# Full-row second score product and token-ordered values in a hybrid attention layer

## The chip, the cores and the metric

The kernel runs on one core of a Trainium2 chip. The metric is the device time of one execution in microseconds (us). Inputs are float32; every large matrix product is carried out in a split form, in which a float32 operand is written as a high and a low part of the type float32r.

## The reference

One layer of a bidirectional encoder over 1024 tokens of width 1024. What matters here is the middle line, a mixture of dilated windows in three groups of eight heads (group 0: dilation 1, group 1: dilation 4, group 2: dilation 16).

```python
h = rmsnorm(x, attn_norm_g)
proj = h @ w_in                        # 1024 x 8096, split into the parts below
(c_q, c_kv, k_rope, z_mla, q_dil, k_dil, v_dil, z_dil, g_mla, g_dil) = jnp.split(proj, ...)
a_out = mla_attention(c_q, c_kv, k_rope, ...)            # 8 heads, dense
d_out = dilated_mixture(q_dil, k_dil, v_dil, positions)  # 3 x 8 heads of 64
merged = sigmoid(g_mla + b) * ((a_out * silu(z_mla)) @ w_o_mla) \
       + sigmoid(g_dil + b) * ((d_out * silu(z_dil)) @ w_o_dil)
return rmsnorm(x + merged @ w_out, final_norm_g)

# a dilated group: token t belongs to class t % dilation and sees, within its class,
# keys at most window / (2 dilation) = 64 places away
def to_sub(t):
    return t.reshape(B, L, dilation, H, D).transpose(0, 2, 3, 1, 4)
s = einsum('brhnqd,brhnkd->brhnqk', qb, kb) * D ** -0.5
p = exp(where(valid, s, NEG_INF) - max)                  # den = sum(p), o = p @ v / den
```

The three groups' outputs are then added with the weights of a softmax over their log-denominators.

## The kernel before

**Split products.** `split` makes the high part by a copy on ScalarE and the low part by a subtraction on VectorE or GpSimd. `mm3` (lines 67 to 71) adds three matmuls, high by high, low by high and high by low; wherever it is used, the profile has rows of L69, L70 and L71. Transposed normalised inputs stay in SBUF as `hT_h` and `hT_l`, 128 partitions x 8 chunks x 1024 tokens each. `dma` (line 65) issues every transfer from SyncE's queue, so all of them are rows of SP and L65, in one order.

**Order.** The program is written as functions, one after the other, and a scheduler with a timeline model places the instructions of each engine by the tiles that they read and write. Inside the attention the order is also written out: `feed` takes so many steps of a generator of other products, `fillers` (the z tiles, the gates and the branches' projections), and sets them behind the latest matmul of the attention (`self.anchor`). `FIRST_FEED` and `FEED` are the tables of these numbers.

**Stages, by the profiled execution.**
- 0 to 40 us: `latent_proj` loads the input and makes the latents; `token_factors` makes the norm's factor of each token, as a row in DRAM (`s_rs`) and back in columns (`rcol`, and by class of four `rcol4`).
- about 50 to 266 us: `dil_v`, the values of the dilated heads, for three groups of two "quads" of four heads each. A tile is 128 tokens by 256 columns: eight chunks of the contraction, three matmuls each, with the tokens as the weights of TensorE and the 256 columns of `wv` as the moving operand. In group 1 the 128 tokens of a tile are those of one class, every fourth column of `hT_h` and `hT_l`, so that the rows come out by class. ScalarE and VectorE scale the result into a tile `dv_st` (three buffers), and a store of 128 pieces of 2 KB takes it to DRAM (`s_dv`). Group 0 runs until about 112 us, group 1 until 218, group 2 until 266. Between them stand the steps of `latents`, the up-projections of the MLA branch, which go through two buffers in PSUM (`pl`) and two in SBUF (`mla_st`).
- 266 to 530 us: `dil_qk`, rotated queries and keys, stored in DRAM as `s_dq` and `s_dk`, with a high and a low part for groups 0 and 1.
- 532 to 876 us: `dil_attention`, in four pairs of heads; in each pair, two heads of group 0, two of group 1 (`dil_head`), and both heads of group 2 together (`dil_classes`), then `combine`. "Change of pair" below means the place where a pair's group 2 ends and the next pair's group 0 begins.
- 876 to 1250 us: the MLA attention, 1250 to 1397 us: the output projection.

**A head of group 0 or 1** loads three operands, each in two buffers: the queries `op_b` (two parts, high and low, of 64 rows x 1024 tokens), the keys `op_a` (the high part in rows 0 to 63, the low part in rows 64 to 127) and the values `op_c`. The high part of the queries is copied by ScalarE from rows 0 to 63 into rows 64 to 127 (line 628), so that one matmul over 128 rows (line 641) gives high queries times both parts of the keys. A second one (line 642) over 64 rows adds low queries times high keys. Both have 128 queries as weights and 256 keys as moving columns. There are 16 heads with 8 blocks of queries: 128 pairs of line 641 and line 642. `soft_block` then takes mask, maximum and exponential on VectorE (line 613) and ScalarE (line 614); line 649 transposes the result, and line 662 (group 0) or 670 (group 1) multiplies by the values.

Of the kernel before, what the change touches and what calls it, by code (L numbers as in the profile page):

```python
# [10 lines left out]
F32 = mybir.dt.float32  # L11
# [18 lines left out]
# steps of other products given between those of the attention  # L30
FIRST_FEED = 19
FEED = (1.9, 1.35, 1.2, 1.25, 2, 3, 1.1, 1.1)
# numbers of buffers
# [4 lines left out]
# column tiles of w_in that come out transposed  # L38
# [11 lines left out]
class Net:  # L50
# [22 lines left out]
    def split(self, raw, h, l, sub):  # L73
        """raw float32 -> h + l, both of float32r, exactly."""
        self.nc.scalar.copy(out=h, in_=raw)  # L75
        sub.tensor_tensor(out=l, in0=raw, in1=h.bitcast(F32), op=ALU.subtract)  # L76

# [10 lines left out]
    def proj_half(self, w, half, pool):  # L88
        """One column tile times 512 tokens: [128, 512] in PSUM."""
        return run_all(self.proj_steps(w, half, pool))  # L90

    def proj_steps(self, w, half, pool):
        """proj_half in steps of a chunk of the contraction."""
        ps = pool.tile([128, 512], F32, name="pj")
        t = slice(half * 512, half * 512 + 512)
        for kc in range(8):
            self.mm3(ps, w[0][:, kc], w[1][:, kc], self.hTh[:, kc, t], self.hTl[:, kc, t], kc == 0, kc == 7)
            if kc < 7:
                yield
        return ps  # L100

# [10 lines left out]
    def rsqrt(self, x, scale, pool, n):  # L112
        """(x * scale + EPS) ** -0.5 of [128, n], by Newton's method from the exponent's half."""
# [12 lines left out]
    def rsqrt_half(self, x, pool):  # L126
        """(2 x) ** -0.5 of [128, 1], with its sign turned: a step of Newton's method from the square root."""
        v = self.nc.vector
        y, u = (pool.tile([128, 1], F32, name=f"rs_{c}") for c in "yu")
        self.nc.scalar.activation(out=y, in_=x, func=AF.Sqrt, scale=2.0)  # L130
        v.reciprocal(out=y, in_=y)
        v.scalar_tensor_tensor(out=u, in0=y, scalar=x, in1=y, op0=ALU.mult, op1=ALU.mult)
        v.scalar_tensor_tensor(out=y, in0=u, scalar=-1.5, in1=y, op0=ALU.add, op1=ALU.mult)
        return y

    def load_x(self, half, kc, xp):
        """(x g)^T in two parts; the tokens' factors are applied to the products."""
# [8 lines left out]
    def latent_proj(self, lp, wl, xp, pj):  # L146
        """c_q, c_kv and the shared rotary key by token, before their factors, and the sums of squares."""
# [33 lines left out]
    def token_factors(self, xp, pp):  # L181
        """The input norm's factor of each token: in columns, by class of four, and on all partitions."""
# [15 lines left out]
        self.dma(self.rcol4, flat.rearrange("(k m r) -> m r k", k=2, r=4))  # L198

    def tables(self, tp):  # L200
        """cos and sin: rows p % 32 of the dilated heads' angles, rows p % 16 of MLA's."""
# [26 lines left out]
    def rope(self, pa, pb, cos, sin, tp):  # L228
        """Rotated halves of [128, 512] from two PSUM tiles."""
# [22 lines left out]
    def latents(self, up, lp, tp, pj):  # L252
        """The latents' norms and the up-projections, by 512 tokens."""
# [3 lines left out]
        for half in range(2):  # L257
            c512 = slice(half * 512, half * 512 + 512)
            # with the tokens' factors r: r * (r r mean + eps) ** -0.5
# [24 lines left out]
            # the shared rotary key: halves at rows 0..15 and 32..47  # L284
# [25 lines left out]
            # queries  # L310
# [6 lines left out]
            # keys  # L317
# [7 lines left out]
            # values  # L325
# [10 lines left out]
    def dil_v(self, g, quad, tp, pj):  # L336
        """Values of four dilated heads, by token (of groups 1 and 2, by class)."""
# [10 lines left out]
        for t in range(8):  # L348
            ps = pj.tile([128, 512], F32, name="pj")[:, :256]
            for kc in range(8):  # L350
                wh, wl = w[kc // 4]
                if g != 1:
                    sl = slice(128 * t, 128 * t + 128)
                    th, tl = self.hTh[:, kc, sl], self.hTl[:, kc, sl]
                else:
                    r4, k2 = t // 2, t % 2
                    th, tl = (x[:, kc].rearrange("p (m r) -> p r m", r=4)[:, r4, 128 * k2:128 * k2 + 128] for x in (self.hTh, self.hTl))
                self.mm3(ps, th, tl, wh[:, kc % 4], wl[:, kc % 4], kc == 0, kc == 7)
            pv = ps.rearrange("p (h d) -> p h d", d=64)
            f = self.rcol4[:, t // 2, t % 2:t % 2 + 1] if g == 1 else self.rcol[:, t:t + 1]  # L360
            if g < 2:
# [3 lines left out]
                r = 128 * t + (64 if g == 0 else 0)  # L365
                self.dma(self.dv[g][r:r + 128, quad * 512:quad * 512 + 512], st.rearrange("p h a d -> p (h a d)"))
# [5 lines left out]
    def dil_qk(self, g, quad, which, tp, pj):  # L372
        """Rotated queries or keys of four dilated heads."""
# [7 lines left out]
        for half in range(2):  # L381
# [3 lines left out]
            for c in range(2):  # L385
# [7 lines left out]
                else:  # L393
                    # classes 2b, then classes 2b + 1
# [6 lines left out]
        for c in range(2):  # L401
            for p in range(len(st[c])):
                for j in range(4):
                    # [head][part][half][32][tokens]
                    self.dma(dst[quad * 4 + j, p, c, :, off:off + S], st[c][p][32 * j:32 * j + 32])

# [1 line left out]
    def piece(self, src, j, half, zj, br, x, z):  # L408
        """A piece of a branch's output times silu(z), in two parts."""
# [6 lines left out]
    def fillers(self, pj):  # L416
        """Matrix products that run between those of the attention."""
# [69 lines left out]
    def o_proj(self, i, dt, half, w, w0, js, br, t, pp, w3=None):  # L487
        """Products of a branch's output projection, [128, 512], and the gate's tanh."""
# [77 lines left out]
    def mla_factors(self, pair, half, den, ap, pp):  # L566
        """1 / (2 denominator) of two heads' 512 queries, a row a token: silu's tanh form lacks the half."""
# [31 lines left out]
    def av_sum(self, av, out, ap, view=None):  # L599
        """The two halves (of V's high and low parts) of [128, 512] added."""  # L600
# [8 lines left out]
    def soft_block(self, s, mask, p, st, g, hh, b):  # L609
        """p = exp(0.125 (s + mask) - max), with -max and the sum kept."""  # L610
# [5 lines left out]
    def dil_head(self, g, h, hh, st, num, ap, pp):  # L616
        nc = self.nc
        mm = nc.tensor.matmul
        rows = slice(64 * hh, 64 * hh + 64)
# [5 lines left out]
        # products: the queries' high part, twice, with both parts of the keys; their low part with the keys' high one  # L625
        for p in range(2):
            self.dma(q[0:64, p], self.dq[g][h, p].rearrange("c r t -> (c r) t"))
        nc.scalar.copy(out=q[64:128, 0], in_=q[0:64, 0])
        self.dma(k[:, :S + pad], self.dk[g][h].rearrange("a c r t -> (a c r) t"))
        self.dma(vv[:, :nch], self.dv[g].rearrange("(c p) x -> p c x", p=128)[:, :, 128 * h:128 * h + 128])  # L630
        for u in range(4):
            # two blocks of 128 queries, each with 256 keys
            s = self.sp.tile([128, 512], F32, name="s_ps", bufs=NB_S)
            p = ap.tile([128, 512], F32, name="p", bufs=3)
            for i in range(2):
# [6 lines left out]
                self.anchor = mm(s[:, o], q[0:64, 1, qs], k[0:64, ks], start=False, stop=True)  # L642
# [3 lines left out]
            # key chunk, query block -> place  # L646
# [6 lines left out]
            if g == 0:  # L653
                # four query blocks' places, between zeros
# [16 lines left out]
            if u % 2 == 1:  # L671
                if g == 0:
                    self.av_sum(av, num[rows, 512 * (u // 2):512 * (u // 2) + 512], ap)
                else:
                    nv = num[rows].rearrange("p (m r) -> p r m", r=4)
                    self.av_sum(av, nv[:, u - 1:u + 1], ap, lambda x: x.rearrange("p (r m) -> p r m", r=2))

    def dil_classes(self, pair, st, num, ap, pp):
        """Two heads of group 2: each class of 64 tokens sees itself; operands with zeros off the diagonal blocks."""
# [68 lines left out]
    def combine(self, pair, st, nums, ap, dx, pp):  # L748
# [7 lines left out]
        # a row has 64 tokens, of both heads  # L756
# [46 lines left out]
    def output(self, pp):  # L803
        nc, a, tc = self.nc, self.a, self.tc
        v = nc.vector
        with tc.tile_pool(name="w3", bufs=1) as w3p, tc.tile_pool(name="wo", bufs=1) as wp, tc.tile_pool(name="mg", bufs=1) as mp:
# [5 lines left out]
            # what is left of the projection, in an order in which two weight tiles are enough  # L812
# [28 lines left out]
            with tc.tile_pool(name="fin", bufs=2) as tp:  # L841
                gf = tp.tile([128, D], F32, name="g_fin", bufs=1)
                self.dma(gf, a["g_final"].partition_broadcast(128))
                # against the sign of rsqrt_half
                nc.gpsimd.tensor_scalar(out=gf, in0=gf, scalar1=-1.0, scalar2=None, op0=ALU.mult)
                for t in range(8):
# [6 lines left out]
                    for i, (lo, hi) in enumerate(zip(cuts, cuts[1:])):  # L853
# [7 lines left out]
                        # half of mean + eps  # L861
# [10 lines left out]
    def run(self):  # L872
        tc, nc = self.tc, self.nc
        with ExitStack() as ctx:
# [15 lines left out]
            self.rcol4 = cp.tile([128, 4, 2], F32, name="rcol4")  # L890
# [138 lines left out]
```

## Time and profile before

| | |
|---|---|
| median of three runs | 1396.82 us |
| the three runs | 1396.5, 1396.82, 1403.9 us |
| the profiled execution | time 1396.5 us, span 1396.5 us |
| TensorE (PE) busy | 1353.5 us, 7101 matmuls |
| weight loads (PEld) busy | 1157.6 us |
| VectorE, ScalarE, GpSimd busy | 675.7, 595.0, 454.9 us |
| moved by DMA | 204.67 MB, mean 147 GB/s |

The profiled execution's time and its span agree to the digit. "Busy" of PE runs from a matmul's start to its modelled end; matmuls overlap there, so the distance from start to start tells how fast they really follow each other. A row of the timeline is: start (us from the span's begin), duration (us), engine, line, operation, output tile, inputs, their partitions x elements, and in brackets how long the engine stood idle before it and what released it. A group's row is: line, engine, operation, shapes, count, then busy time (us) and mean duration of one (ns), then idle time before. A row of windows gives the stretch, its length, and for PE, weight loads, DVE, ACT and POOL the busy time with the count of instructions; then the granted clock of TensorE, the mean busy share of the DMA engines, and GB/s. A row of DMA issues gives the transfer, the engine that issues it, the count, the size of one, and the median time in us from issue to landing.

### The profile page before, as it was taken

What the parts mean: (1) busy time and instruction counts of PE and PEld (TensorE: products, weight loads), DVE (VectorE), ACT (ScalarE), POOL (GpSimd) and SP (SyncE); (2) the same over time, 40 slices, a digit from 0 to 9 for tenths busy, and PEclk for the clock granted to TensorE, in tenths of its full rate; (3) what the DMA queues carried; (4) which work ended last, traced back from release to release, by engine and by line L of the source; (5) the groups of instructions that cost most, each with busy time, mean ns of one, the idle gap of its engine ahead of it and who ended that gap; (6) DMA issues with size and microseconds to landing.
All of it is one profiled execution on the core that took longest, in us unless ns stands there. A gap on an engine that the chain in (4) does not pass through costs nothing.

```text
span 1396.5 us, 19590 instructions
## 1 busy us (share of the span) xinstructions
PE 1353.5 (97%) x7101; PEld 1157.6 (83%) x7101; DVE 675.7 (48%) x1340; ACT 595.0 (43%) x1246; POOL 454.9 (33%) x302
## 2 busy tenths in 40 slices
PE   8999999999999999999999999899999998999998
PEld 7989999988888887777877778778888887887786
DVE  7472421022222222457556565666656566667722
ACT  6432213123221324545555464455556554554322
POOL 2151201277546744433513021122102012026522
PEclk9999999999999999999999999999999999999999
DMA  9756344456526444455566666645434354126332
GB/s 325 213 173 241 109 159 148 128 143 193 142 82 166 115 114 132 128 145 159 163 162 187 162 188 150 157 134 154 126 86 120 93 145 153 54 91 209 131 99 82
DMA packets 127248, 204.67 MB, mean 147 GB/s; under 512 B 37480, under 2 KB 66736, under 8 KB 125296
## 3 DMA queue, kind: packets, MB, share of 16 engines
q1 hardware_dynamic: 127152, 203.43, 49.8%
q8 instruction: 56, 0.92, 0.3%
q14 instruction: 40, 0.33, 0.1%
HBM read 134.63 MB, written 68.75 MB: 146 GB/s over the span
## 4 chain that ended last, share of the span: by engine, by line
PE 81%; DMA 9%; DVE 5%; issue 3%; ACT 1%; SPq 1%; POOL 0%; DVEq 0%; ACTq 0%; POOLq 0%
PE pj L69 20%; PE pj L71 19%; PE pj L70 19%; PE pt L547 3%; PE s_ps L642 2%; PE pt L649 2%; PE av L556 2%; PE av L555 2%; PE s_ps L69 2%; PE s_ps L70 2%; PE s_ps L71 2%; PE s_ps L641 2%; PE av L662 1%; DMA gate<-s_zs 1%; PE av L670 1%
## 5 line engine op out<-in xcount | busy, mean ns | idle before, releaser
L69 PE MATMUL pj<-hT_h,w_h 128*128 128x512 f32 x768 | 313.8, 409 | 0.7 <-DVE zg_z L429 0.7
L76 POOL TENSOR_TENSOR w_l<-w_raw,w_h 128x1024 fp32r<-128x1024 f32 (+1 forms) x70 | 166.4, 2380 | 454.0 <-ACT w_h L75 392.9
L71 PE MATMUL pj<-hT_h,w_l 128*128 128x512 f32 x768 | 301.2, 392 | 0.0
L70 PE MATMUL pj<-hT_l,w_h 128*128 128x512 f32 x768 | 300.9, 392 | 0.0
L234 DVE TENSOR_TENSOR rope_m<-pj,cs_d 128x512 f32<-128x512 f32 x96 | 61.8, 685 | 242.9 <-PE pj L71 238.3
L76 DVE TENSOR_TENSOR pt_l<-pt,pt_h 128x512 fp32r<-128x512 f32 x192 | 131.7, 686 | 90.0 <-ACT pt_h L75 88.4
L71 PEld LDWEIGHTS pj<-hT_h,w_l 128*128 128x128 f32 x768 | 144.8, 189 | 31.2
L75 ACT CAST pt_h<-pt 128x512 fp32r<-128x512 f32 x192 | 112.1, 584 | 133.6 <-PE pt L547 49.4
L69 PEld LDWEIGHTS pj<-hT_h,w_h 128*128 128x128 f32 x768 | 145.3, 189 | 26.5 <-DVE zg_z L429 1.0
L70 PEld LDWEIGHTS pj<-hT_l,w_h 128*128 128x128 f32 x768 | 145.5, 189 | 24.6
L70 PE MATMUL pj<-w_l,hT_h 128*128 128x256 f32 x384 | 123.5, 322 | 0.0
L71 PE MATMUL pj<-w_h,hT_l 128*128 128x256 f32 x384 | 122.9, 320 | 0.0
L69 PE MATMUL pj<-w_h,hT_h 128*128 128x256 f32 x384 | 122.3, 319 | 0.0
L75 ACT CAST w_h<-w_raw 128x1024 fp32r<-128x1024 f32 (+1 forms) x70 | 72.3, 1035 | 70.7 <-PE pj L70 53.5
L536 ACT ACTIVATE p<-s_ps,m_nm 128x512 f32<-128x512 f32 x128 | 87.4, 697 | 33.9 <-PE pt L547 16.9
L530 DVE TENSOR_REDUCE m_nm<-s_ps 128x1 f32<-128x512 f32 x128 | 86.7, 685 | 25.9 <-PE s_ps L71 23.6
L71 PEld LDWEIGHTS pj<-w_h,hT_l 128*128 128x128 f32 x384 | 91.4, 238 | 0.5
L69 PEld LDWEIGHTS pj<-w_h,hT_h 128*128 128x128 f32 x384 | 91.2, 238 | 0.7
L70 PEld LDWEIGHTS pj<-w_l,hT_h 128*128 128x128 f32 x384 | 91.4, 238 | 0.3
L547 PE MATMUL pt<-consts,p 128*128 128x128 f32 x512 | 78.5, 276 | 5.5 <-ACT av_t L578 4.7
L614 ACT ACTIVATE p<-p,d_st 128x256 f32<-128x256 f32 x128 | 64.4, 504 | 43.9 <-DVE d_st L613 43.7
L613 DVE CUSTOM_DVE_ANT_0 p<-s_ps,masks 128x256 f32<-128x256 f32 x128 | 51.6, 417 | 60.4 <-PE s_ps L642 35.4
(235 smaller groups left out, 2605.7 us busy)
## 6 DMA issues: line engine op xcount, KB each, us to landing
w_raw<-wt SPq DMA_DIRECT2D x48, 512.0 KB, 3.8
s_dq<-dq_st SPq DMA_DIRECT2D x80, 128.0 KB, 2.6
s_dk<-dq_st SPq DMA_DIRECT2D x80, 128.0 KB, 2.5
gate<-s_gt SPq DMA_DIRECT2D x34, 256.0 KB, 4.0
s_dv<-dv_st SPq DMA_DIRECT2D x32, 256.0 KB, 3.9
op_b<-s_dq SPq DMA_DIRECT2D x32, 256.0 KB, 5.6
s_gt<-zg_t SPq DMA_DIRECT2D x32, 256.0 KB, 2.0
w_raw<-wv SPq DMA_DIRECT2D x12, 512.0 KB, 5.1
```

The lines of the kernel that those rows point to most:

```text
L69: mm(out, lh, rh, start=start, stop=False)
L70: mm(out, lh, rl, start=False, stop=False)
L71: return mm(out, ll, rh, start=False, stop=stop)
L75: self.nc.scalar.copy(out=h, in_=raw)
L76: sub.tensor_tensor(out=l, in0=raw, in1=h.bitcast(F32), op=ALU.subtract)
L234: v.tensor_tensor(out=mi, in0=p, in1=tab, op=ALU.mult)
L530: v.tensor_reduce(out=nm[:, hh, qb, kb:kb + 1], in_=s, axis=AX.X, op=ALU.max, negate=True)
L536: nc.scalar.activation(out=p[:, 512 * kb:512 * kb + 512], in_=ss[kb], func=AF.Exp, bias=nm[:, hh, qb, 2:3], accum_out=den[:, hh, qb, kb:kb ...
L547: self.anchor = nc.tensor.transpose(pt[:, o:o + 128], P[b2][:, 128 * kc:128 * kc + 128], self.ident)
L555: nc.tensor.matmul(a_out, vv[:, kc], ph[:, s], start=kc == 0, stop=False)
L613: nc.vector.tensor_tensor_reduce(out=p, in0=s, in1=mask, op0=ALU.add, op1=ALU.min, scale=-0.125, scalar=3e38, accum_out=nm)
L614: nc.scalar.activation(out=p, in_=p, func=AF.Exp, scale=-1.0, bias=nm, accum_out=den)
```

## The change

**Values of group 1.** A tile is now 128 successive tokens, as in the other groups, so the weights lie together in SBUF and the factor is the token's own column of `rcol`. The store puts the rows in order of class: a tile has 32 tokens of each of the four classes, and its 128 pieces of 2 KB go to four stretches of 32 rows of `s_dv`. `rcol4` and its transfer are gone (its tile, line 890, and the transfer, line 198).

**Score products of groups 0 and 1.** The queries' tile is loaded twice, into rows 0 to 63 and into rows 64 to 127, with both parts each time; the copy on ScalarE is gone. The second product runs over all 128 rows: low queries times both parts of the keys, so the low-by-low term is added. A head issues two transfers for its queries as before, now of 512 KB each instead of 256 KB.

The core of the diff; the rest of it takes out comments and blank descriptions, so that line numbers after it are 1 to 3 lower.

```diff
 def token_factors(self, xp, pp):
         self.dma(self.R, flat.partition_broadcast(128))
-        self.dma(self.rcol4, flat.rearrange("(k m r) -> m r k", k=2, r=4))

 def dil_v(self, g, quad, tp, pj):
-                if g != 1:
-                    sl = slice(128 * t, 128 * t + 128)
-                    th, tl = self.hTh[:, kc, sl], self.hTl[:, kc, sl]
-                else:
-                    r4, k2 = t // 2, t % 2
-                    th, tl = (x[:, kc].rearrange("p (m r) -> p r m", r=4)[:, r4, 128 * k2:128 * k2 + 128] for x in (self.hTh, self.hTl))
-                self.mm3(ps, th, tl, wh[:, kc % 4], wl[:, kc % 4], kc == 0, kc == 7)
+                sl = slice(128 * t, 128 * t + 128)
+                self.mm3(ps, self.hTh[:, kc, sl], self.hTl[:, kc, sl], wh[:, kc % 4], wl[:, kc % 4], kc == 0, kc == 7)
             pv = ps.rearrange("p (h d) -> p h d", d=64)
-            f = self.rcol4[:, t // 2, t % 2:t % 2 + 1] if g == 1 else self.rcol[:, t:t + 1]
+            f = self.rcol[:, t:t + 1]
             if g < 2:
...
-                r = 128 * t + (64 if g == 0 else 0)
-                self.dma(self.dv[g][r:r + 128, quad * 512:quad * 512 + 512], st.rearrange("p h a d -> p (h a d)"))
+                x = slice(quad * 512, quad * 512 + 512)
+                if g == 0:
+                    dst = self.dv[0][128 * t + 64:128 * t + 192, x]
+                else:
+                    dst = self.dv[1].rearrange("(r m) x -> m r x", r=4)[32 * t:32 * t + 32, :, x]
+                self.dma(dst, st.rearrange("p h a d -> p (h a d)"))

 def dil_head(self, g, h, hh, st, num, ap, pp):
         q = self.op.tile([128, 2, S], F32R, name="op_b", bufs=2)
...
-        for p in range(2):
-            self.dma(q[0:64, p], self.dq[g][h, p].rearrange("c r t -> (c r) t"))
-        nc.scalar.copy(out=q[64:128, 0], in_=q[0:64, 0])
+        for rows in (slice(0, 64), slice(64, 128)):
+            self.dma(q[rows], self.dq[g][h].rearrange("p c r t -> (c r) p t"))
...
                 mm(s[:, o], q[:, 0, qs], k[:, ks], start=True, stop=False)
-                self.anchor = mm(s[:, o], q[0:64, 1, qs], k[0:64, ks], start=False, stop=True)
+                self.anchor = mm(s[:, o], q[:, 1, qs], k[:, ks], start=False, stop=True)
```

Where the order moves. First ScalarE at the second change of pair (near 705 us in the profile before): L711 and L722 belong to group 2, L628 are the copies of the next two heads' queries, L75 and L431 belong to fillers, L754 to the combination, L614 to the next heads' exponentials. Before:

```order
L711 ACTIVATE p<-p 128x512 x2
L722 COPY pt_h<-pt 128x512
L628 COPY op_b<-op_b 64x1024 x2
L722 COPY pt_h<-pt 128x512
L75 CAST w_h<-w_raw 128x1024
L431 ACTIVATE zg_t<-zg_z 128x512
L754 COPY av_t<-pt 96x128
L614 ACTIVATE p,d_st<-p,d_st 128x256 x4
```

and after:

```order
L709 ACTIVATE p<-p 128x512 x2
L720 COPY pt_h<-pt 128x512 x2
L75 CAST w_h<-w_raw 128x1024
L430 ACTIVATE zg_t<-zg_z 128x512
L752 COPY av_t<-pt 96x128
L613 ACTIVATE p,d_st<-p,d_st 128x256 x4
```

The two copies no longer stand between the two evacuations of group 2's transposes; the rest keeps its order.

Second SyncE's queue at the first change of pair (near 616 us): the loads of the next two heads' values (`s_dv_68`), queries (`s_dq_62`) and keys (`s_dk_65`) of group 0 among fillers' transfers and those of the combination (`s_sd`). Before:

```order
L65 DMA w_raw<-wt 128x1024
L65 DMA op_c<-s_dv_68 128x9x128
L65 DMA op_b<-s_dq_62 64x1024
L65 DMA s_zs<-zg_t 128x512
L65 DMA op_b<-s_dq_62 64x1024 x3
L65 DMA op_c<-s_dv_68 128x9x128
L65 DMA s_sd<-av_t 96x128
L65 DMA c_sn<-s_sd 16x4x64
```

and after:

```order
L65 DMA w_raw<-wt 128x1024
L65 DMA op_c<-s_dv_68 128x9x128
L65 DMA op_b<-s_dq_62 64x2x1024
L65 DMA s_zs<-zg_t 128x512
L65 DMA op_b<-s_dq_62 64x2x1024 x3
L65 DMA op_c<-s_dv_68 128x9x128
L65 DMA s_sd<-av_t 96x128
L65 DMA op_a<-s_dk_65 128x1152
L65 DMA c_sn<-s_sd 16x4x64
```

The four loads of queries keep their places and have twice the size; the second head's keys, which were issued after the combination's transfers, now stand among them.

Third TensorE inside the second pair (near 637 us): L641 and L642 (after: L639 and L640) are the two score products, L649 (L647) the transposes, L69 to L71 a filler's step, L662 (L660) the product with the values. Before:

```order
L71 MATMUL pj<-hT_h,w_l 128x512
L641 MATMUL s_ps<-op_a,op_b 128x256
L642 MATMUL s_ps<-op_a,op_b 128x256
L641 MATMUL s_ps<-op_a,op_b 128x256
L642 MATMUL s_ps<-op_a,op_b 128x256
L649 MATMUL pt<-consts,p 128x128 x2
L69 MATMUL pj<-hT_h,w_h 128x512
```

and after:

```order
L71 MATMUL pj<-hT_h,w_l 128x512
L639 MATMUL s_ps<-op_a,op_b 128x256
L640 MATMUL s_ps<-op_a,op_b 128x256
L639 MATMUL s_ps<-op_a,op_b 128x256
L640 MATMUL s_ps<-op_a,op_b 128x256
L639 MATMUL s_ps<-op_a,op_b 128x256
L640 MATMUL s_ps<-op_a,op_b 128x256
L647 MATMUL pt<-consts,p 128x128 x2
L69 MATMUL pj<-hT_h,w_h 128x512
```

A third score pair now stands ahead of the transposes. Up to the end of `dil_qk`, TensorE's order is the same before and after.

More of the change, by code (lines that the diff above doesn't have):

```diff
@@ L618, in dil_head @@
         mm = nc.tensor.matmul
-        rows = slice(64 * hh, 64 * hh + 64)
+        out = slice(64 * hh, 64 * hh + 64)
         pad = 128 if g == 0 else 0
@@ L672, in dil_head @@
                 if g == 0:
-                    self.av_sum(av, num[rows, 512 * (u // 2):512 * (u // 2) + 512], ap)
+                    self.av_sum(av, num[out, 512 * (u // 2):512 * (u // 2) + 512], ap)
                 else:
-                    nv = num[rows].rearrange("p (m r) -> p r m", r=4)
+                    nv = num[out].rearrange("p (m r) -> p r m", r=4)
                     self.av_sum(av, nv[:, u - 1:u + 1], ap, lambda x: x.rearrange("p (r m) -> p r m", r=2))
@@ L889, in run @@
             self.rcol = cp.tile([128, 8], F32, name="rcol")
-            self.rcol4 = cp.tile([128, 4, 2], F32, name="rcol4")
             self.ht_pool = ExitStack()
```

## The prediction
> **What bounds the kernel now.** I read the page first: span, busy shares, the slices, the chain of work that ended last.
>
> ```profile
> span 1396.5 us, 19590 instructions
> PE 1353.5 (97%) x7101; PEld 1157.6 (83%) x7101; DVE 675.7 (48%) x1340; ACT 595.0 (43%) x1246; POOL 454.9 (33%) x302
> PE   8999999999999999999999999899999998999998
> PE 81%; DMA 9%; DVE 5%; issue 3%; ACT 1%; SPq 1%; POOL 0%; DVEq 0%; ACTq 0%; POOLq 0%
> ```
>
> TensorE is busy in 1353.5 of 1396.5 us and carries 81% of the chain. "Busy" counts a matmul from its start to its modelled end, though, and matmuls overlap. So the next thing to read is the distance from one start to the next, in the timeline, at the two places that the change touches. The profiled execution's 1396.5 us is also the fastest of the three times, so nothing measurable lies around the span; the median is 0.3 us above it.
>
> **Part 1, values of group 1 in token order.** The same product, 128x256 from eight chunks of three matmuls, runs for group 1 with weights picked every fourth token, and for group 2 with weights that lie together. First the load of weights alone (windows 176 to 186 and 230 to 240 us), then the first and last of 13 and of 26 back-to-back starts, then the stretch in which group 1 runs.
>
> ```profile
> L70 PEld LDWEIGHTS pj<-w_l,hT_h 128*128 128x128 f32 x15 | 5.0, 330 | 0.0
> L70 PEld LDWEIGHTS pj<-w_l,hT_h 128*128 128x128 f32 x28 | 5.4, 192 | 0.0
> 140.80 0.39 PE L71 MATMUL pj<-w_h,hT_l 128*128 128x256 f32 x1
> 143.83 0.39 PE L69 MATMUL pj<-w_h,hT_h 128*128 128x256 f32 x1
> 229.80 0.28 PE L69 MATMUL pj<-w_h,hT_h 128*128 128x256 f32 x1
> 232.92 0.28 PE L71 MATMUL pj<-w_h,hT_l 128*128 128x256 f32 x1
> 112.20:218.20 106.00, 106.00 (x474) 103.72 (x472) 30.86 (x49) 25.89 (x45) 13.87 (x7) 1.00 0.44 163
> ```
>
> Strided: 3.03 us for 13 steps, 0.233 each, paced by a load of 330 ns. Together: 3.12 us for 26 steps, 0.120 each. Group 1 has 2 quads x 8 tiles x 8 chunks x 3 = 384 such matmuls, and TensorE has no gap in their 106 us, so the product is on the path: 384 x 0.113 = 43 us saved.
>
> [...]
>
> What is late next. Between these matmuls stand the latents' steps, each an evacuation on ScalarE and VectorE into one of two buffers and a 512 KB store.
>
> ```profile
> 106.94 0.60 ACT L306 ACTIVATE mla_st<-pj 128x512 fp32r<-128x512 f32 x1 [2.25 <-DMA s_qn<-mla_st]
> s_kn<-mla_st SPq DMA_DIRECT2D x8, 512.0 KB, 3.1
> s_dv<-dv_st SPq DMA_DIRECT2D x17, 256.0 KB, 2.0
> w_raw<-wv SPq DMA_DIRECT2D x4, 512.0 KB, 5.1
> ```
>
> ScalarE already waits for these stores where TensorE runs at the fast pace. A step costs 0.6 (ScalarE), by estimate as long on VectorE, some 0.5 for the issue, and the landing, shared by two buffers: with a landing of 3.1 us, 2.4 us; with 5.1 (the longest of these rows), 3.4. TensorE will bring a step every 2.5 to 3.1 us (14 to 16 matmuls of 0.12, and 3 or 6 of 512 columns at some 0.23). In this stretch stand 22 steps (7 keys and values of the first half of the tokens, 15 of the second): an excess of 0 to 0.7 us each, 0 to 15 us lost. The bytes of 106 us come in about 69, so 163 GB/s becomes 250 and landings will be above 3.1; I take 6 us. Net of part 1: 43 - 6 = 37.
>
> The store itself keeps its 128 pieces of 2 KB, only their places change. No row shows a store with this pattern: at 2.0 us it costs nothing; at 10.9, the longest median in the attention (row below), a tile takes (1 + 0.3 + 10.9) / 3 buffers = 4.1 us against 2.9 of matmuls, 16 x 1.2 = 19 us. I take 0, since size and count of the pieces are those of the 2.0 row. Scaling by the token's own column instead of the class's changes no instruction. The removed transfer of class factors goes ahead of a weight load for which ScalarE, and after it TensorE, wait.
>
> ```profile
> op_c<-s_mv SPq DMA_DIRECT2D x2, 512.0 KB, 10.9
> 67.39 0.67 SPq L65 DMA_DIRECT2D rcol<-s_rs  x1
> PE pj L278 <- DVE lat_l L282: 2.4, 1, 2.4
> ```
>
> Its issue took 0.67 us; between 0 and the whole 2.4 us of wait may go. I take 1.
>
> **Part 2, the second score product on 128 rows.** Three pairs in a row, two weight loads of these, a lone pair, and the first start and the end of ten full-row matmuls.
>
> ```profile
> 588.36 0.40 PE L71 MATMUL pj<-hT_h,w_l 128*128 128x512 f32 x1
> 588.59 0.28 PE L641 MATMUL s_ps<-op_a,op_b 128*128 128x256 f32 x1
> 588.80 0.38 PE L642 MATMUL s_ps<-op_a,op_b 64*128 64x256 f32 x1
> 589.11 0.38 PE L641 MATMUL s_ps<-op_a,op_b 128*128 128x256 f32 x1
> 590.36 0.39 PE L670 MATMUL av<-pt_h,op_c 128*128 128x256 f32 x1
> 588.36 0.19 PEld L641 LDWEIGHTS s_ps<-op_a,op_b 128*128 128x128 f32 x1
> 588.80 0.18 PEld L642 LDWEIGHTS s_ps<-op_a,op_b 64*128 64x128 f32 x1 [0.25 <-issue]
> 596.20 0.28 PE L641 MATMUL s_ps<-op_a,op_b 128*128 128x256 f32 x1
> 596.72 0.39 PE L670 MATMUL av<-pt_h,op_c 128*128 128x256 f32 x1
> 580.98 0.28 PE L662 MATMUL av<-pt_h,op_c 128*128 128x256 f32 x1
> 582.12 0.39 PE L71 MATMUL pj<-hT_h,w_l 128*128 128x512 f32 x1
> ```
>
> Between full-row matmuls the load runs ahead (588.36 for the matmul at 588.59). At the 64-row one it starts only with its matmul, and the next full-row one waits again. Three pairs take 1.77 us, 0.59 each; a lone pair 0.52; two full-row matmuls of 256 columns 2 x 0.114 = 0.23. With 0.575 between the two: 128 pairs x 0.345 = 44 us.
>
> [...]
>
> The product streams the same 256 columns, and the added low-by-low term costs no instruction. What replaces the copy on ScalarE (16 x 1.046 us, off TensorE's path except where it blocks the queue) is twice the bytes: 1 MB a head instead of 512 KB, in two issues as before, and the first product now waits for both halves of the rows. The tight places are the three changes of pair, where both buffers come free only after group 2. Copies of the two heads, and the first product, at the third, second and first change:
>
> ```profile
> 787.71 1.04 ACT L628 CAST op_b<-op_b 64x1024 fp32r<-64x1024 f32 x1 [2.22 <-issue]
> 790.23 1.04 ACT L628 CAST op_b<-op_b 64x1024 fp32r<-64x1024 f32 x1 [0.87 <-issue]
> 789.57 0.36 PE L641 MATMUL s_ps<-op_a,op_b 128*128 128x256 f32 x1
> 704.83 1.04 ACT L628 CAST op_b<-op_b 64x1024 fp32r<-64x1024 f32 x1 [1.36 <-DMA op_b<-s_dq]
> 707.43 0.36 PE L641 MATMUL s_ps<-op_a,op_b 128*128 128x256 f32 x1
> 619.70 1.04 ACT L628 CAST op_b<-op_b 64x1024 fp32r<-64x1024 f32 x1 [4.46 <-DMA op_b<-s_dq]
> 620.79 0.38 PE L641 MATMUL s_ps<-op_a,op_b 128*128 128x256 f32 x1 [1.70 <-ACT op_b L628]
> 660.35 1.09 SPq L65 DMA_DIRECT2D op_b<-s_dq  x2
> 664.45 1.05 ACT L628 CAST op_b<-op_b 64x1024 fp32r<-64x1024 f32 x1 [0.26 <-DMA op_b<-s_dq]
> 668.62 0.38 PE L641 MATMUL s_ps<-op_a,op_b 128*128 128x256 f32 x1
> 532.00:876.00 344.00, 336.38 (x1775) 268.97 (x1773) 195.59 (x482) 181.86 (x434) 109.10 (x85) 0.99 0.60 160
> ```
>
> A copy starts when the first 256 KB have landed; the second head's follows 2.5 us (512 KB) later. The missing 768 KB are worth 3.8 us: ready at 791.5 where the product stood at 789.57 (1.9 late), at 708.6 against 707.43 (1.2), at 623.5 against 620.79 (2.7). Sum 6 us; between 0 (the queue may be emptier by then) and 12 (twice), I take 7. The order gives no more cover than before: 18, 18 and 24 matmuls of 512 columns stand between the last product of group 2 and that score product, in both kernels. Inside a pair, a load goes out at 660.35 and landed first at 664.45; with 3.8 more, and the keys queued behind it on SP, it is ready near 671 where the product, now some 2.8 us (8 pairs x 0.345) earlier, wants it at 666. This is the tightest of eight such heads: 0 to 5 us each, 0 to 40 in all; I take 8, one in four as late as this. In the other direction, the copies leave ScalarE's queue, where they held the evacuation behind them (the 1.70 us above, and smaller ones): 4 us back, between 0 and 6. The scheduler also sets some score pairs next to each other and moves transfers of the combination by a place or two; I count that as 0, within 3 us to either side (a wait of TensorE for ScalarE or VectorE of the size of the 1.70 us above, twice), since the other engines have room. VectorE and ScalarE, busy 196 and 182 of 344 us, stay at or below two thirds of about 311. Net of part 2: 44 - 15 + 4 = 33.
>
> Sum: 1396.5 - 37 - 1 - 33 = 1325.5, say **1326 us**.
>
> **Rivals.**
> - Everything is hidden: landings stay short and the order has room. 1396.5 - 43 - 44 - 1 = 1308. For it: TensorE loses nothing at the fast pace of group 2, and the copies' 4 us may come on top (1304); against: the three changes of pair above.
> - The transfers take more: 15 us lost on the latents' stores instead of 6, and 35 in the attention instead of 15: 29 more, about 1355. For it: the late row at 619.70; against: a share of 0.60.
> - Weight loads of full rows don't run ahead for these operands: the score part gains 0 and the larger loads still cost 11: 1396.5 - 37 - 1 + 11 = 1370.
> - The stride isn't what slows the loads: 1396.5 - 33 - 1 = 1363. Against: two products alike in all but the stride.
> - Slower than before: the queries' loads become the bound of the attention. 7 MB more over the 55 MB (160 GB/s x 344 us) of this stretch; it costs all that the change gains only if the stretch takes 382 us instead of 311, that is, if the transfers saturate at 163 GB/s. Today's 160 GB/s fill a share of 0.60, so full would be about 267 GB/s, 233 us.
>
> **How the numbers follow.** A measurement tells about 0.5%, 7 us, from no change. Chances: my sum (1316 to 1339) 0.58; all hidden 0.18; transfers take more 0.14; no overlap of loads 0.04; stride not the cause 0.03; slower 0.02; nothing 0.01. From 1303 to 1357 lie the first two and most of the third, over 0.8. Faster by over 0.5%: 0.97; within: 0.01; slower: 0.02.
>
> **What would show it.** Right: group 1's weight loads at 192 ns and starts 0.12 apart; the stretch of 106 us near 69; score matmuls all 128 rows, starts 0.12 apart; new waits of TensorE for the queries' loads at the changes of pair, and of ScalarE for the latents' stores. Wrong: second score loads that still start with their matmul, stores of values that land late, or the attention's DMA share near 1 with TensorE waiting at every head.

## The result, and the profile after

The changed kernel takes 1334.79 us (median of four runs, 1333.66 to 1338.08) against 1396.9 before: a ratio of 0.9552, 95% interval 0.9519 to 0.9585. In the second set of runs below it gave 0.9562 (0.9525 to 0.9598). 1326 was forecast, 1303 to 1357 as the range.

The page of the kernel after: span, busy time, TensorE's slices, and the chain that ended last by engine.

```profile
span 1332.5 us, 19561 instructions
PE 1275.5 (96%) x7101; PEld 1108.2 (83%) x7101; DVE 670.5 (50%) x1340; ACT 577.7 (43%) x1230; POOL 454.9 (34%) x302
PE   8999999999999999989999989999999999998998
PE 64%; DMA 12%; DVE 6%; issue 3%; SPq 2%; ACT 1%; POOL 0%; DVEq 0%; ACTq 0%; POOLq 0%
```

TensorE is still the bound, busy in 1275.5 of 1332.5 us. Its part of the chain fell from 81% to 64% and that of transfers rose from 9% to 12%, but the parts shown add up to 88% here and to 100% before, so the chain does not tell how much of the gain is now waiting; the stages do. From one stage's first matmul to the next one's, the two profiled executions (1396.5 and 1332.5 us) compare as follows.

| stage | before | after | difference | forecast |
|---|---|---|---|---|
| to the end of the values | 265.8 | 225.5 | -40.3 | -38 |
| queries and keys | 266.6 | 266.6 | 0 | 0 |
| dilated attention | 344.4 | 323.3 | -21.1 | -33 |
| MLA attention and output | 519.7 | 517.1 | -2.6 | 0 |

**Values of group 1.** The weight load in 114 to 176 us, the whole of group 1, and the first and last of 14 starts in a row:

```profile
L70 PEld LDWEIGHTS pj<-w_l,hT_h 128*128 128x128 f32 x122 | 23.2, 190 | 0.5
112.89:177.43 64.54, 64.53 (x475) 61.17 (x473) 30.33 (x47) 23.77 (x42) 12.09 (x6) 1.00 0.67 247
144.95 0.28 PE L70 MATMUL pj<-w_l,hT_h 128*128 128x256 f32 x1
146.51 0.28 PE L71 MATMUL pj<-w_h,hT_l 128*128 128x256 f32 x1
```

The load takes 190 ns instead of 330, starts are 0.12 us apart, and the stretch of 106.0 us is 64.5. TensorE has no gap in it, though 247 GB/s pass instead of 163.

**Scores.** The first four pairs of the attention, and two of their weight loads:

```profile
492.08 0.28 PE L639 MATMUL s_ps<-op_a,op_b 128*128 128x256 f32 x1
492.19 0.28 PE L640 MATMUL s_ps<-op_a,op_b 128*128 128x256 f32 x1
...
492.91 0.28 PE L640 MATMUL s_ps<-op_a,op_b 128*128 128x256 f32 x1
492.08 0.19 PEld L640 LDWEIGHTS s_ps<-op_a,op_b 128*128 128x128 f32 x1
492.20 0.19 PEld L639 LDWEIGHTS s_ps<-op_a,op_b 128*128 128x128 f32 x1
```

Eight starts in 0.83 us, 0.12 apart; each load begins with the matmul before it. So the pace came as forecast. What it ran into stands in the waits of TensorE in the attention (waiting engine and line, what it waited for, then us in total, times, longest):

```profile
PE s_ps L639 <- DVE d_st L612: 5.6, 5, 2.7
PE s_ps L639 <- DMA op_b<-s_dq: 4.5, 1, 4.5
PE s_ps L639 <- DMA op_a<-s_dk: 3.8, 3, 2.8
PE s_ps L639 <- issue: 3.0, 2, 1.7
PE pj L69 <- DVE zg_z L428: 2.1, 3, 1.5
PE av L660 <- DVE pt_l L76: 1.8, 3, 1.0
PE pt L647 <- DVE pt_l L76: 1.5, 1, 1.5
PE s_ps L703 <- POOL op_b L689: 0.5, 1, 0.5
```

Together 22.8 us. The same view of before sums to 8.4; these are its rows for VectorE and for the exponentials of ScalarE:

```profile
PE pt L649 <- ACT p L614: 2.4, 2, 1.7
PE s_ps L641 <- DVE d_st L613: 0.8, 1, 0.8
PE pj L69 <- DVE zg_z L429: 0.7, 1, 0.7
```

After the change, loads of queries and keys hold 8.3 us, and probably the 3.0 of "issue" too, since its two waits stand at the first product after the second and the third change of pair. VectorE holds 11.0, where it held 1.5. ScalarE, which held 4.6 (with the 1.7 for a copy of queries and 0.5 for an evacuation), holds nothing. One of these waits also leaves something behind it. The first change of pair, its wait, and the granted clock (third number from the end) during and after it:

```profile
574.84 0.36 PE L639 MATMUL s_ps<-op_a,op_b 128*128 128x256 f32 x1 [4.54 <-DMA op_b<-s_dq]
570.00:576.40 6.40, 1.86 (x10) 1.60 (x9) 1.76 (x7) 1.53 (x5) 2.52 (x2) 0.89 1.04 248
576.40:582.00 5.60, 5.60 (x24) 5.17 (x23) 1.38 (x3) 1.10 (x6) 0.00 (x0) 0.51 0.99 196
492.08:815.40 323.32, 299.98 (x1774) 262.11 (x1772) 191.26 (x482) 167.33 (x420) 108.36 (x85) 0.97 0.74 193
```

The queries land 4.5 us late, with the DMA engines full (share 1.04). In the 5.6 us after that TensorE is busy throughout, at a clock of 0.51: it loses another 2.7 us. Summed over stretches of 4 us (busy time times the missing part of the clock), the attention loses 9.1 us in this way; before it lost 5.0.

### The profile page after: what moved, and what is told of

Same layout as the page of the kernel before. It is cut to its first block, busy times and chain, and to the rows that moved or that the text cites. A ratio compares the mean times of both kernels' runs of the same rounds, so it can differ in the third digit from the quotient of the medians.

```text
span 1332.5 us, 19561 instructions
## 1 busy us (share of the span) xinstructions
PE 1275.5 (96%) x7101; PEld 1108.2 (83%) x7101; DVE 670.5 (50%) x1340; ACT 577.7 (43%) x1230; POOL 454.9 (34%) x302
## 4 chain that ended last, share of the span: by engine, by line
PE 64%; DMA 12%; DVE 6%; issue 3%; SPq 2%; ACT 1%; POOL 0%; DVEq 0%; ACTq 0%; POOLq 0%
PE pj L69 15%; PE pj L71 15%; PE pj L70 15%; PE pt L546 3%; DMA op_a<-s_dk 2%; PE av L555 2%; PE av L554 2%; SPq L65 2%; DMA s_sd<-av_t 2%; PE s_ps L69 2%; PE s_ps L70 2%; PE s_ps L71 2%; PE pt L647 1%; DMA gate<-s_zs 1%; PE av L668 1%
## 5 line engine op out<-in xcount | busy, mean ns | idle before, releaser
L69 PE MATMUL pj<-hT_h,w_h 128*128 128x512 f32 x768 | 314.9, 410 | 2.2 <-DVE zg_z L428 2.1
L71 PE MATMUL pj<-hT_h,w_l 128*128 128x512 f32 x768 | 301.8, 393 | 0.0
L71 PEld LDWEIGHTS pj<-hT_h,w_l 128*128 128x128 f32 x768 | 145.4, 189 | 31.7
L69 PEld LDWEIGHTS pj<-hT_h,w_h 128*128 128x128 f32 x768 | 145.8, 190 | 27.7 <-DVE zg_z L428 3.0
L75 ACT CAST pt_h<-pt 128x512 fp32r<-128x512 f32 x192 | 112.0, 584 | 116.5 <-PE pt L546 48.2
L70 PE MATMUL pj<-w_l,hT_h 128*128 128x256 f32 x384 | 109.2, 284 | 0.0
L71 PE MATMUL pj<-w_h,hT_l 128*128 128x256 f32 x384 | 109.0, 284 | 0.0
L69 PE MATMUL pj<-w_h,hT_h 128*128 128x256 f32 x384 | 109.0, 284 | 0.0
L75 ACT CAST w_h<-w_raw 128x1024 fp32r<-128x1024 f32 (+1 forms) x70 | 72.3, 1035 | 72.9 <-PE pj L70 59.4
L535 ACT ACTIVATE p<-s_ps,m_nm 128x512 f32<-128x512 f32 x128 | 87.4, 697 | 30.6 <-PE pt L546 19.1
L69 PEld LDWEIGHTS pj<-w_h,hT_h 128*128 128x128 f32 x384 | 73.2, 191 | 1.1
L70 PEld LDWEIGHTS pj<-w_l,hT_h 128*128 128x128 f32 x384 | 73.3, 191 | 0.8
L71 PEld LDWEIGHTS pj<-w_h,hT_l 128*128 128x128 f32 x384 | 73.1, 190 | 0.7
```

Of the source, the lines that this page charges most:

```text
L69: mm(out, lh, rh, start=start, stop=False)
L70: mm(out, lh, rl, start=False, stop=False)
L71: return mm(out, ll, rh, start=False, stop=stop)
L535: nc.scalar.activation(out=p[:, 512 * kb:512 * kb + 512], in_=ss[kb], func=AF.Exp, bias=nm[:, hh, qb, 2:3], accum_out=den[:, hh, qb, kb:kb ...
```

## The experiments

Three sets, each with its own runs of the kernel before; ratios are to those.

**One part at a time.** `values_only` puts the score part back, `scores_only` the values part.

```diff
# values_only, on the changed kernel
-        for rows in (slice(0, 64), slice(64, 128)):
-            self.dma(q[rows], self.dq[g][h].rearrange("p c r t -> (c r) p t"))
+        for p in range(2):
+            self.dma(q[0:64, p], self.dq[g][h, p].rearrange("c r t -> (c r) t"))
+        nc.scalar.copy(out=q[64:128, 0], in_=q[0:64, 0])
...
-                self.anchor = mm(s[:, o], q[:, 1, qs], k[:, ks], start=False, stop=True)
+                self.anchor = mm(s[:, o], q[0:64, 1, qs], k[0:64, ks], start=False, stop=True)
```

> The kernel after the change with its score part put back: single loads of the queries, ScalarE's copy, 64-row second product. Theory (the two parts act in different stages and do not touch each other): the values' stage takes 40 us less, as in the trace of after, and the rest stays as before, 1396.9 - 41 = 1356 us, 1353 to 1360. Rival (part of the 21 us saved in the attention comes from the earlier values, or the denser values' stage pushes transfers into later stages): outside 1350 to 1363.

Measured: 1358.18 us against 1400.93, ratio 0.9691 (0.9667 to 0.9715): 42.8 us less, where the theory has 41.

> The kernel after the change with its values part put back: group 1 strided by class, class factors, store by rows. Theory (additive): 1396.9 - 23 = 1374 us, 1371 to 1378, and the same new waits of TensorE for the queries' loads at the changes of pair. Rival (the parts help or hinder each other): the two kernels' gains do not sum to the 62 us of the whole within 4 us.

Measured: 1377.73 us, ratio 0.9821 (0.9793 to 0.9849). The gains, 42.8 and 23.2 us, sum to 66; 62 was measured for the whole. By the ratios it is 4.9% against 4.5%, a difference of 0.4% where the three intervals together allow some 0.5%. So they add up as far as can be told; a few us lost between the parts are not excluded. The attention of scores_only shows the wait for the queries' load again, 4.9 us.

**The bytes without the product, and the product without the bytes.** `loads_alone` is the changed kernel with the 64-row product; `zero_rows` is the changed kernel with single loads:

```diff
# loads_alone
-                self.anchor = mm(s[:, o], q[:, 1, qs], k[:, ks], start=False, stop=True)
+                self.anchor = mm(s[:, o], q[0:64, 1, qs], k[0:64, ks], start=False, stop=True)
# zero_rows: two fixed tiles in turn, also for the queries of group 2
+        self.qb = [self.op.tile([128, 2, S], F32R, name="op_b", bufs=2) for _ in range(2)]
+        for x in self.qb:
+            nc.gpsimd.memset(x[64:128, 1].bitcast(F32), 0.0)
...
-        for rows in (slice(0, 64), slice(64, 128)):
-            self.dma(q[rows], self.dq[g][h].rearrange("p c r t -> (c r) p t"))
+        for p in range(2):
+            self.dma(q[0:64, p], self.dq[g][h, p].rearrange("c r t -> (c r) t"))
+        nc.scalar.copy(out=q[64:128, 0], in_=q[0:64, 0])
```

> The kernel after the change, but the second product again over 64 rows: it has the doubled loads of the queries and no copy, and none of the gain of the full-row product. Theory (the doubled bytes are what took back a part of the gain, some 10 to 15 us net of the copies): 1366 us, 1361 to 1372, that is 5 to 16 above values_only. Rival (the bytes are hidden, the loss is from another order of score pairs, transposes and exponentials): 1352 us, 4 below values_only, since the copies are gone.

Measured: 1368.0 us, ratio 0.9765 (0.9739 to 0.9791), 9.8 us above values_only, as the theory of the bytes has it. But they cost otherwise than by waits. The whole attention of values_only, then of loads_alone, and three stretches of loads_alone after a wait of 1.48 us at the first product after a change of pair:

```profile
493.20:838.77 345.57, 337.60 (x1774) 269.79 (x1772) 195.76 (x482) 181.51 (x434) 109.00 (x85) 0.98 0.59 159
```
```profile
492.92:848.93 356.01, 346.58 (x1773) 275.97 (x1772) 194.71 (x483) 169.29 (x421) 109.29 (x85) 0.95 0.67 176
759.96 0.37 PE L639 MATMUL s_ps<-op_a,op_b 128*128 128x256 f32 x1 [1.48 <-issue]
760.00:764.00 4.00, 4.00 (x9) 2.29 (x10) 1.30 (x6) 1.75 (x6) 0.00 (x0) 0.52 1.04 203
764.00:768.00 4.00, 4.00 (x17) 3.71 (x17) 0.00 (x0) 0.05 (x1) 0.00 (x0) 0.50 1.07 313
768.00:772.00 4.00, 4.00 (x12) 3.07 (x12) 1.28 (x3) 0.60 (x2) 0.00 (x0) 0.50 0.53 167
```

TensorE's waits sum to 9.2 us here and 8.0 in values_only, hardly more. Summed over stretches of 4 us as above, the slow clock takes 16.2 us against 6.0, and that is the whole difference. It shows in all four runs: their mean clock is 0.977 to 0.980, that of values_only 0.983 to 0.987.

> The kernel after the change with the full-row second product, but each half of the queries is loaded once, as before the change: the two buffers of the queries are fixed tiles whose low part has zeros in rows 64 to 127, set once, and ScalarE copies the high part as before the change. The low-by-low term is left out, as before the change. Theory (bytes took the gain back): 1334.8 - 12 = 1322 us, 1316 to 1328, no wait of TensorE over 2.5 us for the queries' loads. Rival (the order is to blame, not the bytes): 1333 to 1340, the copies costing up to 5 more.

Measured: 1327.58 us, ratio 0.9475 (0.9451 to 0.95), and 0.9489 (0.9463 to 0.9515) when it ran again as `zero_again` (0.9475, within 0.003, was expected). On the scale of the first set the first is 1324 us, as the theory has it. It beats the changed kernel by about 0.8%, 11 us; between the two profiled executions it is 8.1 us, 6.2 of them in the attention. The row of its attention and its largest waits there:

```profile
490.73:807.85 317.12, 294.34 (x1773) 258.15 (x1772) 195.90 (x483) 180.93 (x435) 111.42 (x85) 0.98 0.66 175
PE s_ps L641 <- DVE d_st L612: 6.0, 2, 3.3
PE pt L649 <- ACT p L613: 4.0, 2, 2.5
PE s_ps L641 <- DMA op_a<-s_dk: 2.5, 1, 2.5
PE pj L69 <- DVE zg_z L428: 2.1, 1, 2.1
```

Against values_only, which has the same bytes and copies, it saves 30.6 us by the runs and 28.5 in the attention. Yet its waits are 22.3 us against 8.0. So with the bytes gone, the faster product still pays 14 us in waits, 11 of them for VectorE and ScalarE (17.9 against 6.7). The rival was right in that much.

**The second set.** `after_again` is the changed kernel, for comparison.

> The changed kernel once more, to stand beside the others of this set: ratio to before 0.9552, within 0.003.

Measured: 1340.33 us against 1403.79, ratio 0.9562.

> The changed kernel with the store of group 1's values by rows in token order: the class order is left out, group 1 works on rows in a wrong order, and everything else is the same. Theory (the class order of the store costs nothing, since pieces, bytes and issue stay): within 2 us of after_again. Rival (rows spread over four stretches land later and hold up the tiles): 5 us or more below after_again.

```diff
-                    dst = self.dv[1].rearrange("(r m) x -> m r x", r=4)[32 * t:32 * t + 32, :, x]
+                    dst = self.dv[1][128 * t:128 * t + 128, x]
```

Measured: 1341.27 us, ratio 0.9563 (0.9526 to 0.96), 0.9 us above after_again: the class order of the store costs nothing that can be told.

> The changed kernel with the weights of the values picked at a step: every second token in group 0, every fourth in group 1, every eighth in group 2; rows of values are left in those orders, so that the later stages work on permuted values. It measures the weight load alone. [...] Rival (it pays by the length of the step): over 400 ns at step 8, about 260 at step 2, the whole over 1450.

```diff
-                sl = slice(128 * t, 128 * t + 128)
+                n = (2, 4, 8)[g]
+                c, m = t * n // 8, 128 * (t % (8 // n))
+                x = [y[:, kc].rearrange("p (m r) -> p r m", r=n)[:, c, m:m + 128] for y in (self.hTh, self.hTl)]
```

Measured: 1421.56 us, in one run. The weight load alone at steps of two, four and eight tokens (mean ns after the comma):

```profile
L70 PEld LDWEIGHTS pj<-w_l,hT_h 128*128 128x128 f32 x73 | 14.3, 196 | 0.0
L70 PEld LDWEIGHTS pj<-w_l,hT_h 128*128 128x128 f32 x96 | 31.4, 327 | 0.1
L70 PEld LDWEIGHTS pj<-w_l,hT_h 128*128 128x128 f32 x97 | 32.8, 338 | 0.0
```

Step two is free here (196 against 190 to 192 ns without a step), step four takes 327, step eight hardly more (338); starts are 0.12, 0.233 and 0.24 us apart. So here the price begins between a step of two values and one of four, and going on to eight adds 11 ns. The rival, by which the load pays by the length of the step, put over 400 ns on step eight and over 1450 us on the whole; neither came. A step of three was not tried, and why the price begins where it does is not shown by these rows.

> zero_rows with more filler steps behind the score products (2.3 instead of 1.9 a step in group 0, 1.6 instead of 1.2 in group 1): fillers then end earlier and less is left for the MLA attention. Theory (what is still lost in the attention is TensorE waiting for VectorE's masks and subtractions after denser score products): TensorE's waits in the attention fall from 22 us to 12 or less, and the whole by 5 to 10 us against zero_rows, 1318 to 1323 on the scale of before at 1397. Rival (the waits come with the changes of pair and the transfers, whatever stands between the score products, or come back in the MLA attention): within 3 us of zero_rows or above it.

```diff
-FEED = (1.9, 1.35, 1.2, 1.25, 2, 3, 1.1, 1.1)
+FEED = (2.3, 1.35, 1.6, 1.25, 2, 3, 1.1, 1.1)
```

Measured: 1345.34 us, ratio 0.9614 (0.9566 to 0.9662), by the ratios 1.4% or 19 us slower than zero_rows; between the profiled executions it is 14.6 us. 24 filler steps moved into the attention, which grew by 18.4 us (317.1 to 335.5), its waits fell only from 22.3 to 19.4, with 7.6 of them now for the fillers' own VectorE step, and the MLA attention, which still runs about as many filler products (606 matmuls against 600), did not get shorter (356.5 to 361.2 us). All that follows the dilated attention is 4.7 us shorter together. The expectation failed: more fillers are not what the waits lack.

**The third set.**

> zero_rows without ScalarE's copy: the high part of the queries is loaded into both halves, the low part once, 768 KB a head between the 512 of zero_rows and the 1024 of the change. Theory (bytes at the changes of pair cost, some 11 us for 512 KB a head, less a few us for the copies that go): 0 to 4 us above zero_again. Rival (the copies on ScalarE are what still holds TensorE, by its waits of 4.0 us for exponentials and 1.3 for a copy): 4 to 6 us below it.

```diff
-        nc.scalar.copy(out=q[64:128, 0], in_=q[0:64, 0])
+        self.dma(q[64:128, 0], self.dq[g][h, 0].rearrange("c r t -> (c r) t"))
```

Measured: 1325.18 us against 1329.42 of zero_again, ratios 0.9462 (0.9434 to 0.9489) and 0.9489 (0.9463 to 0.9515). The sign is the rival's, but the intervals overlap: undecided.

> zero_rows with the combination's products with the broadcast weights (24 of 128x512) on GpSimd instead of VectorE. Theory (VectorE's queue is held by these products while their weights are still on the way from DRAM, and the masks behind them, and TensorE behind those): TensorE's waits for VectorE's masks fall from 6.0 us to about 3, what is left being the masks' own load at the start, and the whole falls by 3 to 6 us against zero_again. Rival (VectorE is short of time in any case, or GpSimd's longer products delay the combination): within 2 us of it.

```diff
-                v.tensor_tensor(out=nums[g][:, c], in0=nums[g][:, c], in1=r, op=ALU.mult)
+                nc.gpsimd.tensor_tensor(out=nums[g][:, c], in0=nums[g][:, c], in1=r, op=ALU.mult)
```

What led to it are two rows of zero_rows: the combination's product on VectorE waits 4.8 us for its weights from DRAM, and a microsecond later TensorE's wait for a mask behind it ends.

```profile
595.63 0.69 DVE L798 TENSOR_TENSOR num<-num,bc 128x512 f32<-128x512 f32 x1 [4.81 <-DMA bc<-s_rr]
596.72 0.39 PE L641 MATMUL s_ps<-op_a,op_b 128*128 128x256 f32 x1 [3.25 <-DVE d_st L612]
```

Measured: 1326.97 us, ratio 0.9468 (0.9432 to 0.9503), 2.4 us below zero_again, less than can be told. TensorE's largest waits in the attention of zero_pool:

```profile
PE s_ps L641 <- ACT p L613: 4.2, 1, 4.2
PE pt L649 <- ACT p L613: 3.6, 2, 2.2
PE s_ps L641 <- DVE d_st L612: 2.9, 1, 2.9
PE s_ps L641 <- ACT zg_t L430: 2.8, 1, 2.8
```

The wait for masks fell from 5.6 us to 2.9, as the theory has it, and the one left is the masks' own load at the start. But a wait of 4.2 us for ScalarE came in its place, and the sum stayed (22.6 in zero_again, 22.4 here). The place was right, the gain was not.

> The changed kernel with both score products over rows 0 to 63: high queries times high keys, then low queries times high keys; high queries times low keys are left out. Theory (a load can't run ahead when the number of rows changes from one matmul to the next): with 64 rows in both, starts inside a pair are 0.12 us apart, as with 128 in both. Rival (a load of 64 rows never runs ahead): 0.29 to 0.31 apart, as in the kernel before.

```diff
-                mm(s[:, o], q[:, 0, qs], k[:, ks], start=True, stop=False)
-                self.anchor = mm(s[:, o], q[:, 1, qs], k[:, ks], start=False, stop=True)
+                mm(s[:, o], q[0:64, 0, qs], k[0:64, ks], start=True, stop=False)
+                self.anchor = mm(s[:, o], q[0:64, 1, qs], k[0:64, ks], start=False, stop=True)
```

Measured: 1351.05 us, in one run. Its first pairs, and the filler behind them:

```profile
492.12 0.38 PE L639 MATMUL s_ps<-op_a,op_b 64*128 64x256 f32 x1
492.35 0.28 PE L640 MATMUL s_ps<-op_a,op_b 64*128 64x256 f32 x1
492.47 0.28 PE L639 MATMUL s_ps<-op_a,op_b 64*128 64x256 f32 x1
...
493.06 0.28 PE L640 MATMUL s_ps<-op_a,op_b 64*128 64x256 f32 x1
493.26 0.50 PE L69 MATMUL pj<-hT_h,w_h 128*128 128x512 f32 x1
```

Among 64-row products the starts are 0.12 us apart, as among full-row ones. Only the first (0.23) and the one ahead of the full-row filler (0.20) take longer. The slow pace of before (0.31 us from start to start, 588.80 to 590.36) was the switch of rows, twice in each pair, and not the 64 rows.

## Why the prediction was right, and where it was off

- **Values: right.** 384 matmuls went from 88.0 us of start-to-start time to 46.3, 41.7 against 43 forecast. The 6 us for the latents' stores did not come: ScalarE waits for them more often, but TensorE not once in group 1; a wait of 2.9 us for an evacuation stands at the end of group 0 instead, where the wait of 2.4 us for `lat_l` fell to 0.6. The two about cancel, so nothing net is seen of the 1 put on the class factors' removal; whether the new wait comes from it was not tested. The store at 0: shown by token_store.
- **Pace of the scores: right at full clock.** The attention fell by 21.1 us, with 14.4 more of waits and 4.1 more of lost clock (9.1 less 5.0): 21.1 + 14.4 + 4.1 = 40 against 44. From values_only to zero_rows, counted in the same way (28.5, 14.3 and nothing), it is 43. Part of the rest are products behind transposes: 0.20 us for the first one of a pair (518.13 to 518.33, say) where 0.115 was put.
- **The larger loads: right in sum, not in kind.** 15 less 4 for the copies, 11 net, was forecast; loads_alone shows 9.8 and zero_rows 11. But it was put as waits alone. At the three changes of pair the waits rose from 2.2 us to 7.5 (4.5 and the 3.0 of "issue"), 5.3 more against 7. Inside pairs the waits for loads, all for keys, rose from 1.0 to 3.8, against 8 more. Most of that is not from the larger loads: 2.8 of it is one wait in the last pair (at 782.54), and zero_rows, with single loads, waits 2.5 us for keys at the same head. About 1 us is left for the larger loads, so this term was far too large. The 4 us for the copies came, as far as the waits show it: those for ScalarE fell from 4.6 us to none. What filled the sum is the slow clock behind the waits, which the forecast did not count: 10 us in loads_alone. In the changed kernel it takes 3.1 us more than in zero_rows (9.1 against 6.0), and in after_again 7.1 more than in zero_again (13.2 against 6.1), so how its 11 us are made up stays in part open.
- **The step that failed: "I count that as 0, within 3 us to either side ... since the other engines have room".** TensorE's waits for VectorE went from 1.5 us to 11.0. Busy shares do not show it: VectorE worked 191 of 323 us. It is held by what it waits for, in order. Two places show it: at the attention's start the masks' load, their first use and TensorE's wait behind it; in the last pair a step of the combination, and a wait of TensorE for a subtraction that stands behind such steps in VectorE's queue:

```profile
495.99 0.35 SPq L65 DMA_DIRECT2D masks<-masks  x1
500.93 0.42 DVE L612 CUSTOM_DVE_ANT_0 p<-s_ps,masks 128x256 f32<-128x256 f32 x1 [7.96 <-DMA s_zs<-zg_t]
501.41 0.39 PE L639 MATMUL s_ps<-op_a,op_b 128*128 128x256 f32 x1 [2.65 <-DVE d_st L612]
746.38 0.21 DVE L772 COPY c_w<-c_sn 16x128 f32<-16x128 f32 x1 [2.90 <-DMA c_sn<-s_sd]
750.21 0.38 PE L660 MATMUL av<-pt_l,op_c 128*128 128x256 f32 x1 [0.99 <-DVE pt_l L76]
```

The second row names a store that this instruction does not read. Of what it reads, the masks came last: they went out at 495.99 and took 4.1 us to land. VectorE was idle 7.6 us there before the change as well, but with the slow pairs TensorE waited only 0.8 us. The other waits for VectorE stand in good part behind the combination's steps, which wait for small transfers from DRAM (the two rows of zero_rows show one more). The larger loads are not needed for it: zero_rows waits 10.7 us for VectorE and 7.2 for ScalarE, values_only 1.7 and 5.0. That this could be had back was not shown: moving one of the waiters off VectorE moved the wait.
- **The rivals.** The transfers did not fill the stage (share 0.74 against 0.60), nor did they take more as that rival has it: nothing on the latents' stores, some 11 us net in the attention. The stride was the cause (strides: 196 ns at step two, 327 at step four), and full-row loads run ahead (the rows at 492.08, starts 0.12 apart). "Everything is hidden" failed by the attention alone.
- **In sum**: -40.3 instead of -38, -21.1 instead of -33, and 2.6 less in the last stages, whose cause stays open. That the total is within 9 us of the forecast is in part luck, since the values and the last stages missed it in the other direction than the attention. Between the two profiles the stages make 64.0 us, and 62.1 lie between the medians: the execution profiled after the change has a time of 1334.28 us beside its span of 1332.5, the one before is on record with 1396.5 for both. That nothing measurable lies around the span, as the prediction has it, is not so in the later runs, before's among them: their time is some 1.8 us above the span.

## What to carry to other kernels

Where matmuls follow each other closely, price them from start to start and look at what alternates between them: beside 0.12 us for the 256 columns streamed, a change in the number of rows at every matmul added 0.19 here (0.31 from start to start in the kernel before), and a step of four values in the weights 0.11 (0.233). When the score pairs went from 0.59 to 0.23 us on the bounding engine, what stood behind them on VectorE came to light: TensorE's waits for it went from 1.5 us to 11.0. So count the idle time of the next engine and its releasers, not its busy share. And where a product only lacked rows, zeros set once were cheaper here than loading the operand twice, by about 11 us (zero_rows against the changed kernel).

## What the runs showed of the hardware

- After some of the waits, though not after each, TensorE's granted clock stood near 0.5 for several us of full work: 0.51 over 5.6 us after 4.54 of waiting here, and 0.50 to 0.52 over 12 us after 1.48 in loads_alone, with TensorE busy throughout by the profile; after 2.65 us at 501.41 it stayed full (1.00 from 501.4 to 505.4). Why it stayed low so long in loads_alone was not found.
- Weight loads ran ahead under a matmul of the same rows, of 128 (changed kernel, 492.08: starts 0.12 us apart) as of 64 (same_rows, 492.35: 0.12), and not across a change from one to the other (before, 588.80: the load starts with its matmul). Such a change cost about 0.1 us where it stood alone (same_rows: 0.23 at 492.12 and 0.20 at 493.06) and some 0.19 where it came at every matmul (before: 0.31 from start to start).
- A weight load of 128 columns of `hT_h` took 190 to 192 ns without a step (changed kernel and before), 196 at a step of two values, 327 to 330 at four (strides and before), and 338 at eight (strides).
